# Feed-forward values and the residual stream turned by VectorE in 32x32 blocks instead of by TensorE

## The chip, the cores and the metric

The kernel runs on one core of one Trainium2 chip. The metric is the device time of one execution in microseconds (us). Engines are named as the profile names them: PE is TensorE (PEld its weight loads), DVE is VectorE, ACT is ScalarE, POOL is GpSimd, SP is the engine that issues most DMAs.

## What is computed

An encoder trunk of two layers on 256 tokens of 2048 channels, all in float32. The attention, state-space and pooling parts stand before the output projection and are not touched by the change:

```python
def hybrid_layer(x, norm1_w, w_in, ..., norm2_w, w_gate, w_up, w_down):
    h = rms_norm(x, norm1_w)
    proj = jnp.matmul(h, w_in).astype(jnp.float32)
    ...
    mix = jnp.concatenate([att, ssd, pool], axis=-1).astype(x.dtype)
    x = x + jnp.matmul(mix, w_out)
    h = rms_norm(x, norm2_w)
    ff = jax.nn.silu(jnp.matmul(h, w_gate)) * jnp.matmul(h, w_up)
    return x + jnp.matmul(ff, w_down)
```

After both layers one more RMSNorm gives the output. The feed-forward width is 5632, eleven pieces of 512.

## The kernel before

**Units and halves.** All weights are cut on the host into units of 128 x 2048 numbers (1 MB), in the order in which they are used. `load(i)` brings unit i from memory into one of 3 `raw` buffers. `prep(h)` (line 135) makes half h of a unit, 128x1024, ready: ACT rounds it to the matmul's format (`whi`, L148), DVE computes what the rounding left (`wlo`, L149). Each product is then three matmuls: rounded by rounded (L321), rounded by rest (L322), rest by rounded (L324). So a unit is two halves, and each half is 12 matmuls of 512 columns. `whi` and `wlo` have 5 buffers each: the buffer that half h gives back when its last matmul is through is filled with half h+5, which PE wants four halves later.

**Order of the work.** It is written out by hand. In step i the program issues, engine by engine: the two `prep` of halves 2i+3 and 2i+4, then `evac(i-1)`, which takes the results of the unit before out of PSUM, then unit i's matmuls. Small jobs are put at a place inside a later step with `at(step, fn, pos=k)`; where such a job has PE work, it is slipped in between the matmuls (`side_slot`). Every engine runs its instructions in the order in which they were issued.

**Token units.** Units of kind `out`, `gate`, `up` and `down` go through `mm_token`: the tokens are the stationary operand (two chunks c of 128 tokens), the weights move, and four units (three in the last part of the feed-forward, `PARTS = (4, 4, 3)`) make one result of 256 tokens x 512 channels, with tokens on the partitions. The next matmul needs channels on the partitions, so the result has to be turned:

- after each `up` unit of a group, `ff_up` (L750) multiplies gate and up to `fv`, and `ff_trans` turns it: 8 PE transposes (L759) against an identity into PSUM banks, then ACT (L764) and DVE (L765) split it into rounded part and rest, `ffp`, the operand of `down`. This is done 11 times a layer;
- after each `out` group, and after each `down` group of the last part in layer 0, `residual` (L204) adds the result to `xs`, and `xtrans_feat` turns it in the same way (L218), with the split in `xpair` (L197 on ACT, L198 on DVE) into `xp`, the operand of the next projections. This is done 4 times for each of three residual sums.

The first two `out` groups are held open: three of their four units run first, then the last unit of group 0 and the last unit of group 1 follow each other directly.

Of the kernel before, what the change touches and what calls it, by code (L numbers as in the profile page):

```python
# [15 lines left out]
F32 = mybir.dt.float32  # L19
F32R = mybir.dt.float32r  # L20
AF = mybir.ActivationFunctionType
# [26 lines left out]
def trunk(ctx, tc, xT, xin, wall, par, fin, dsk, plw, cst, dtab, rcnt, out):  # L48
# [22 lines left out]

    def t3(name, dt=F32):
        return ep.tile([128, 3, T], dt, tag="e", name=name)

    def bank(name):
        return auxp.tile([128, 512], F32, tag="aux", name=name)
# [114 lines left out]
    def xpair(k, l, off, v=None):  # L191
# [6 lines left out]
        DVE.scalar_tensor_tensor(t[:, T:], v, w, t[:, :T].bitcast(F32), op0=ALU.mult, op1=ALU.subtract)  # L198
        st["xp"][k] = t

    def residual(n, accs):
        for c in range(2):
            x = xs[c][:, n * 512:n * 512 + 512]
            DVE.tensor_tensor(x, x, accs[c], op=ALU.add)  # L204
# [5 lines left out]
            q = t2("sq")  # L210
            ACT.activation(q, xs[c][:, n * 512:n * 512 + 512], AF.Square, accum_out=st["ssq"][:, c * 4 + n:c * 4 + n + 1])

    def xtrans_feat(n, l, off, half):
        p = bank("xf")
        for b in range(2):
            f = (4 * n + 2 * half + b) * 128
            for c in range(2):
                PE.transpose(p[:, b * T + c * 128:b * T + c * 128 + 128], xs[c][:, f:f + 128], ident)  # L218
                yield
        for b in range(2):  # L220
            xpair(4 * n + 2 * half + b, l, off, p[:, b * T:b * T + T])

    def rstd_cols():
        r = sm.tile([128, T + 4], F32, name="rbc", bufs=1)
# [519 lines left out]
            del st["plw"], st["rc"]  # L744

    def ff_up(f, accs):
        st["fv"] = []
        for c in range(2):
            v = t2("fv")
            DVE.scalar_tensor_tensor(v, accs[c], st["r"][:, T + c:T + c + 1], st["sg"][c], op0=ALU.mult, op1=ALU.mult)  # L750
            st["fv"].append(v)
        del st["sg"]

    def ff_trans(f, half, fv):
        p = bank("ft")
        for b in range(2):
            o = (2 * half + b) * 128
            for c in range(2):
                PE.transpose(p[:, b * T + c * 128:b * T + c * 128 + 128], fv[c][:, o:o + 128], ident)  # L759
                yield  # L760
        for b in range(2):
            t = t2("ffp", F32R)
            v = p[:, b * T:b * T + T]
            ACT.copy(t[:, :T], v)  # L764
            DVE.tensor_tensor(t[:, T:], v, t[:, :T].bitcast(F32), op=ALU.subtract)  # L765
            st["ff", 4 * f + 2 * half + b] = t

    def fin_load():
        st["fw"] = [t2("fw") for _ in range(4)]
# [27 lines left out]
    def evac(i, acc):  # L797
        u = units[i]
        kind, l, j = u["kind"], u["l"], u["j"]
        if kind == "dt":  # L800
            dt_evac(l, acc)
            at(i + 2, dt_exp, l, pos="b")
            at(i + 3, dt_ln, pos="b")
            at(i + 4, dt_fin, pos="a")
            at(i + 5, dt_cols)
            at(i + 7, cumsums)
            st["mix"] = [None] * 16
        elif kind == "xbc":
            conv(l, j, acc)
            at(i + 2, conv_tap0, l, j, pos="c")  # L810
            at(i + 3, conv_taps, l, j, pos="a")
            at(i + 4, conv_silu, l, j, pos="b")
            if j < 8:
                at(i + 5, xtrans, j)
            elif j == 11:
                at(i + 5, cb, 0)
                at(i + 6, cb, 1)
            if j == HEADS_AT:
                b = i + 2
                for h in range(16):  # L820
                    at(b + h - (0 if h == 0 else 1), row_load, h, pos="a")
                    at(b + h + 1, decay, h, pos="a")
                    at(b + h + 1, decay_exp, h, pos="b")
                    at(b + h + 2, gmat, h, pos="b")
                    at(b + h + 3, ymm, h)
                b += 1
                for g in range(2):
                    at(b + 8 * g + 10, gate_skip, l, g, pos="a")
                    at(b + 8 * g + 11, gate_mul, g, pos="c")
                    at(b + 8 * g + 12, gate_norm, g, pos="b")  # L830
                    at(b + 8 * g + 13, gate2, l, g, 0)
                    at(b + 8 * g + 14, gate2, l, g, 1)
        elif kind == "z":
            if j == 3:
                st["ssd"] = {}
            if j % 4 == 3:
                if i == 3:
                    at(i + 2, z_evac, 0, acc, pos="c")
                else:
                    z_evac(j // 4, acc)  # L840
        elif kind == "v":
            if j % 4 == 3:
                v_evac(j // 4, acc)
        elif kind == "qk":
            pair, m = divmod(j, 6)
            qk_evac(pair, m, acc)
            if m == 5:
                b = i + 3 if pair == 0 else i + 2
                for c in range(2):
                    at(b + c, att_a, pair, c, pos=13)  # L850
                    at(b + c + 1, att_n, pair, c, pos="a")
                    for sl in range(2):
                        at(b + c + 1, att_b, pair, sl, c, pos=5)
                    at(b + c + 2, att_c, pair, c, pos=2)
        elif kind == "u":
            if j == 3:
                pass
            pool_evac(j, acc)
            at(i + 2, pool_mm, l, j, pos=11)
        elif kind == "out":  # L860
            residual(j, acc)
            squares(j)
            at(i + 2, xtrans_feat, j, l, P_N2, 0, pos=2)
            at(i + 2, xtrans_feat, j, l, P_N2, 1, pos=10)
            if j == 3:
                at(i + 3, rstd_cols, pos="b")
        elif kind == "gate":
            st["sg"] = []
            for c in range(2):
                s = t2("sg")  # L870
                ACT.activation(s, acc[c], AF.Silu, scale=st["r"][:, T + c:T + c + 1])
                st["sg"].append(s)
        elif kind == "up":
            ff_up(j, acc)
            fv = st.pop("fv")
            at(i + 2, ff_trans, j, 0, fv, pos=2)
            at(i + 2, ff_trans, j, 1, fv, pos=10)
        elif kind == "down":
            residual(j, acc)
            if u["part"] == len(PARTS) - 1:  # L880
                squares(j)
                if l + 1 < L:
                    at(i + 2, xtrans_feat, j, l + 1, P_N1, 0, pos=2)
                    at(i + 2, xtrans_feat, j, l + 1, P_N1, 1, pos=10)
                    if j == 3:
                        at(i + 3, rstd_cols, pos="b")
                        at(i + 4, rstd_rows, pos=2)
                        at(i + 5, rstd_parity, pos=2)
                else:
                    if j == 0:  # L890
                        ACT.activation(warm, epst, AF.Sqrt)
                        fin_load()
                    if j < 3:
                        fin_weight(j)
            if j == 3:
                for f in range(4 * u["f0"], 4 * (u["f0"] + u["nq"])):
                    del st["ff", f]
# [73 lines left out]
    return c, d.astype(np.float32), rc  # L971


def _feature(w):
    k, n = w.shape[0] // 128, w.shape[1] // 128
    return w.reshape(k, 128, n, 128).transpose(2, 1, 0, 3).reshape(n, 128, k * 128)
# [7 lines left out]
def _pack(inp):  # L984
    out = []
    put = lambda a: out.append(np.ascontiguousarray(a).reshape(-1))
    for l in range(L):
        w = inp["w_in"][l]
        q, k, v, z, xbc, dt, u = np.split(w, np.cumsum([ATT, ATT, ATT, INNER, 1536, 32])[:6], axis=1)
        put(_token(z))  # L990
        dtp = np.zeros((D, 128), np.float32)
        dtp[:, :32] = dt
        put(_feature(dtp))
        put(_feature(xbc)[list(CONV_ORDER)])
        put(_token(v))
        qf, kf = _feature(q), _feature(k)
        for p in range(4):
            put(qf[[p, 4 + p, 8 + p]])
            put(kf[[p, 4 + p, 8 + p]])
        put(_feature(u)[::-1])  # L1000
        rows = [None] * KT
        for n in range(8):
            rows[n] = 4 + n
        for n in range(4):
            rows[MIX_ATT[n]] = n
            rows[MIX_POOL[n]] = 12 + n
        o = _token(inp["w_out"][l].reshape(KT, 128, D)[rows].reshape(D, D))
        for n in range(HELD):
            put(o[n][:3])
        for n in range(HELD):  # L1010
            put(o[n][3])
        put(o[HELD:])
        g, up = _token(inp["w_gate"][l]), _token(inp["w_up"][l])
        gu = np.stack([g, up], axis=1)
        f0 = 0
        for n in PARTS:
            put(gu[f0:f0 + n])
            put(_token(inp["w_down"][l][f0 * 512:(f0 + n) * 512]))
            f0 += n
    return np.concatenate(out)  # L1020

# [36 lines left out]
```

## Time and profile before

| what | value |
|---|---|
| time, median of 3 runs | 2465.73 us (2465.63 to 2467.09) |
| the profiled execution's own time | 2464.96 us |
| its span in the trace | 2463.2 us |
| TensorE clock granted, mean | 0.998 |
| PE busy | 2440.2 us, 99% |
| DVE busy | 1427.1 us, 58% |
| ACT busy | 1186.4 us, 48% |
| memory read | 454.43 MB, 185 GB/s over the span |

A row of a group of instructions gives line, engine, operation, what is written and what is read, shapes and count; after the first bar the summed busy time in us and the mean of one in ns; after the second bar the idle time of the engine just before them in us, and what ended it. A row of a timeline gives start in us, length in us, engine, line, operation and count; in brackets the idle time before it and what ended it. A line number is that of the kernel before; the changed kernel's lines are some 4 higher at the top and 27 higher further down.

### The profile page before, as it was taken

To read this page: it belongs to the slowest core of one execution; us is meant where nothing else is said; L and a number is where in the kernel's file an instruction comes from. 1 tells how busy PE (TensorE), PEld (TensorE's weight loads), DVE (VectorE), ACT (ScalarE), POOL (GpSimd) and SP (SyncE) were. 2 spreads that over 40 slices of the span, in tenths; PEclk is the share of its full clock that TensorE was granted. 3 is DMA by queue.
4 is the path that set the end of the run, shared out by engine and by line. 5 is a ranking of instruction groups with operands and counts; after the bars stand their busy time and mean duration, and the time that the engine had idled before them with its cause. 6 is when DMAs were issued, how large, how long until landed. Compare 5 with 4: busy or idle time off the path is not lost.

```text
span 2463.2 us, 30214 instructions
## 1 busy us (share of the span) xinstructions
PE 2440.2 (99%) x11954; PEld 2029.4 (82%) x11954; DVE 1427.1 (58%) x1791; ACT 1186.4 (48%) x1610; POOL 238.1 (10%) x329
## 2 busy tenths in 40 slices
PE   8999999999999999999999999999999999999997
PEld 7888888888888888888888888888888888888886
DVE  6787765555454555545558787655545545454454
ACT  6576554544444444344555755445544444444443
POOL 2175002000000000000001830020000000000001
PEclk9999999999999999999999999999999999999999
DMA  7565544455555555555454654445555555555553
GB/s 271 200 220 171 175 153 155 172 204 188 188 188 196 193 185 194 189 188 190 173 201 157 225 180 155 165 160 188 187 190 188 188 193 187 194 193 191 188 200 125
DMA packets 67103, 458.57 MB, mean 186 GB/s; under 512 B 7776, under 2 KB 7920, under 8 KB 13328
## 3 DMA queue, kind: packets, MB, share of 16 engines
q1 hardware_dynamic: 63360, 445.27, 50.6%
q0 software_dynamic: 3456, 11.09, 1.6%
q8 instruction: 94, 1.54, 0.3%
q14 instruction: 49, 0.40, 0.0%
q10 hardware_dynamic: 144, 0.26, 0.0%
HBM read 454.43 MB, written 2.16 MB: 185 GB/s over the span
## 4 chain that ended last, share of the span: by engine, by line
PE 98%; DVE 1%; ACT 0%; issue 0%; DMA 0%; POOL 0%; SPq 0%; DVEq 0%; ACTq 0%; POOLq 0%
PE acc L321 25%; PE acc L324 25%; PE acc L322 25%; PE acc L286 11%; PE acc L288 6%; PE ft L759 1%; PE acc L291 1%; PE sc L649 1%; PE op L688 1%; PE pt L673 1%; PE y L569 0%; PE y L567 0%; PE xf L218 0%; DMA raw<-wall 0%; DVE s L656 0%
## 5 line engine op out<-in xcount | busy, mean ns | idle before, releaser
L149 DVE TENSOR_TENSOR wlo<-raw,whi 128x1024 fp32r<-128x1024 f32 (+1 forms) x839 | 1028.0, 1234 | 846.9 <-ACT whi L148 845.7
L148 ACT CAST whi<-raw 128x1024 fp32r<-128x1024 f32 (+1 forms) x839 | 873.5, 1049 | 976.9 <-PE acc L324 832.9
L321 PE MATMUL acc<-whi,xp 128*128 128x512 f32 x1728 | 685.8, 397 | 8.4 <-ACT whi L148 8.4
L324 PE MATMUL acc<-whi,xp 128*128 128x512 f32 x1728 | 685.5, 397 | 0.0
L322 PE MATMUL acc<-wlo,xp 128*128 128x512 f32 x1728 | 674.8, 391 | 0.0
L286 PE MATMUL acc<-xp,whi 128*128 128x512 f32 x1230 | 458.3, 409 | 0.0
L321 PEld LDWEIGHTS acc<-whi,xp 128*128 128x128 f32 x1728 | 326.0, 189 | 77.5 <-ACT whi L148 8.4
L324 PEld LDWEIGHTS acc<-whi,xp 128*128 128x128 f32 x1728 | 326.0, 189 | 70.9
L322 PEld LDWEIGHTS acc<-wlo,xp 128*128 128x128 f32 x1728 | 326.2, 189 | 63.6 <-DVE wlo L149 0.4
L288 PE MATMUL acc<-xp,wlo 128*128 128x256 f32 x1312 | 367.2, 290 | 0.0
L324 PE MATMUL acc<-whi,ffp 128*128 128x512 f32 x704 | 277.3, 394 | 0.0
L321 PE MATMUL acc<-whi,ffp 128*128 128x512 f32 x704 | 277.3, 394 | 0.0
L322 PE MATMUL acc<-wlo,ffp 128*128 128x512 f32 x704 | 274.1, 389 | 0.0
L286 PEld LDWEIGHTS acc<-xp,whi 128*128 128x128 f32 x1230 | 231.3, 188 | 50.4 <-issue 3.2
L288 PEld LDWEIGHTS acc<-xp,wlo 128*128 128x128 f32 x1312 | 248.2, 189 | 14.5 <-issue 0.8
L324 PEld LDWEIGHTS acc<-whi,ffp 128*128 128x128 f32 x704 | 132.2, 188 | 29.5
L321 PEld LDWEIGHTS acc<-whi,ffp 128*128 128x128 f32 x704 | 132.2, 188 | 28.6
L322 PEld LDWEIGHTS acc<-wlo,ffp 128*128 128x128 f32 x704 | 132.3, 188 | 26.2
L451 POOL TENSOR_TENSOR pad<-cd,rbc 128x256 f32<-128x256 f32 x24 | 18.7, 781 | 1019.8 <-DVE cd L274 1019.8
L324 PE MATMUL acc<-whi,mix 128*128 128x512 f32 x256 | 102.7, 401 | 0.0
L321 PE MATMUL acc<-whi,mix 128*128 128x512 f32 x256 | 102.1, 399 | 0.0
L322 PE MATMUL acc<-wlo,mix 128*128 128x512 f32 x256 | 99.8, 390 | 0.0
(183 smaller groups left out, 1584.1 us busy)
## 6 DMA issues: line engine op xcount, KB each, us to landing
raw<-wall SPq DMA_DIRECT2D x417, 1024.0 KB, 4.8
rowb<-rowd POOLq DMA_DIRECT2D x32, 256.0 KB, 3.7
xt<-xT SPq DMA_DIRECT2D x8, 256.0 KB, 7.7
xs<-xin SPq DMA_DIRECT2D x2, 1024.0 KB, 7.9
out<-xs SPq DMA_DIRECT2D x5, 256.0 KB, 3.4
raw<-wall SPq DMA_DIRECT2D x4, 256.0 KB, 5.9
rc<-rcnt POOLq DMA_DIRECT2D x4, 256.0 KB, 5.8
fw<-fin POOLq DMA_DIRECT2D x4, 256.0 KB, 3.6
```

The lines of the kernel that those rows point to most:

```text
L148: ACT.copy(hi[:, c:e], r)
L149: DVE.tensor_tensor(lo[:, c:e], r, hi[:, c:e].bitcast(F32), op=ALU.subtract)
L286: PE.matmul(acc, lhsT=hi, rhs=rhs, start=first, stop=False)
L288: PE.matmul(acc[:, T:], lhsT=lo, rhs=rhs[:, :T], start=False, stop=False)
L291: PE.matmul(acc, lhsT=hi, rhs=rhs, start=False, stop=True)
L321: PE.matmul(a, lhsT=xh, rhs=hi[:, s], start=first, stop=False)
L322: PE.matmul(a, lhsT=xh, rhs=lo[:, s], start=False, stop=False)
L324: PE.matmul(a, lhsT=xl, rhs=hi[:, s], start=False, stop=last)
L649: PE.matmul(p[sl][:, o:o + n], lhsT=q[a, m, c::2], rhs=k[a, m] if m == 0 else k[a, m, c::2], start=True, stop=True)
L673: PE.transpose(p[:, b * 128:b * 128 + 128], s[:, b * 128:b * 128 + 128], ident)
L688: PE.matmul(p[64 * sl:64 * sl + 64, c * 128:c * 128 + 128], lhsT=vs[b][:, h:h + 64], rhs=pt[sl][:, b * 128:b * 128 + 128], start=(b == 0), ...
L759: PE.transpose(p[:, b * T + c * 128:b * T + c * 128 + 128], fv[c][:, o:o + 128], ident)
```

## The change

The 32x32 block transpose of DVE takes the place of the PE transposes for `fv` and `xs`. `move` copies a 128x512 tile by 16 instructions: number (a, b) reads partitions 32a to 32a+31, columns 128b to 128b+127, turns its four 32x32 blocks, and writes partitions 32b to 32b+31, columns 128a to 128a+127. That leaves the channels of each group of 512 in another order on the partitions, and the rows of `w_in`, `w_gate`, `w_up` and `w_down`, the two norm weights and the first input `xT` are put into the same order on the host (`_order`). The transposed tile lies in SBUF, in a buffer of the pool `ep`, and the split into rounded part and rest reads it there, in pieces of 128x128 (four runs of 32 columns) instead of 128x256 from PSUM.

```diff
+    def t3f(name):
+        return t3(name).rearrange("p a b -> p (a b)")[:, :512]
...
+    def move(v, d):
+        for a in range(4):
+            for b in range(4):
+                DVE.transpose(d[32 * b:32 * b + 32, 128 * a:128 * a + 128],
+                              v[32 * a:32 * a + 32, 128 * b:128 * b + 128])
+
+    def turned(d, m):
+        return d.rearrange("p (a m j) -> p m a j", a=4, m=4)[:, m]
+
+    def cols(t):
+        return t.rearrange("p (a j) -> p a j", a=4)
...
-    def xtrans_feat(n, l, off, half):
-        p = bank("xf")
-        for b in range(2):
-            f = (4 * n + 2 * half + b) * 128
-            for c in range(2):
-                PE.transpose(p[:, b * T + c * 128:b * T + c * 128 + 128], xs[c][:, f:f + 128], ident)
-                yield
-        for b in range(2):
-            xpair(4 * n + 2 * half + b, l, off, p[:, b * T:b * T + T])
+    def x_turn(n):
+        st["xd", n] = [t3f("xd") for _ in range(2)]
+        for c in range(2):
+            move(xs[c][:, n * 512:n * 512 + 512], st["xd", n][c])
+
+    def x_split(n, l, off, half):
+        if n == 0 and half == 0:
+            st["xp"] = [None] * KT
+        for m in (2 * half, 2 * half + 1):
+            k = 4 * n + m
+            t = t2("xp", F32R)
+            w = pr[:, l, off + k:off + k + 1]
+            for c in range(2):
+                v = turned(st["xd", n][c], m)
+                hi, lo = (cols(t[:, o + c * 128:o + c * 128 + 128]) for o in (0, T))
+                ACT.activation(hi, v, AF.Copy, scale=w)
+                DVE.scalar_tensor_tensor(lo, v, w, hi.bitcast(F32), op0=ALU.mult, op1=ALU.subtract)
+            st["xp"][k] = t
+        if half:
+            del st["xd", n]
...
     def ff_up(f, accs):
-        st["fv"] = []
+        st["fd"] = []
         for c in range(2):
             v = t2("fv")
             DVE.scalar_tensor_tensor(v, accs[c], st["r"][:, T + c:T + c + 1], st["sg"][c], op0=ALU.mult, op1=ALU.mult)
-            st["fv"].append(v)
+            d = t3f("fd")
+            move(v, d)
+            st["fd"].append(d)
         del st["sg"]
 
-    def ff_trans(f, half, fv):
-        p = bank("ft")
...
+    def ff_split(f, half):
+        for m in (2 * half, 2 * half + 1):
+            t = t2("ffp", F32R)
+            for c in range(2):
+                v = turned(st["fd"][c], m)
+                hi, lo = (cols(t[:, o + c * 128:o + c * 128 + 128]) for o in (0, T))
+                ACT.copy(hi, v)
+                DVE.tensor_tensor(lo, v, hi.bitcast(F32), op=ALU.subtract)
+            st["ff", 4 * f + m] = t
+        if half:
+            del st["fd"]
...
         elif kind == "out":
             residual(j, acc)
             squares(j)
-            at(i + 2, xtrans_feat, j, l, P_N2, 0, pos=2)
-            at(i + 2, xtrans_feat, j, l, P_N2, 1, pos=10)
+            x_turn(j)
+            at(i + 2, x_split, j, l, P_N2, 0, pos=2)
+            at(i + 2, x_split, j, l, P_N2, 1, pos=8)
...
+def _order(n):
+    f = np.arange(n).reshape(n // 512, 4, 4, 32)
+    return f.transpose(0, 2, 1, 3).reshape(n)
```

`down` of the last part in layer 0 is changed as `out` is. Where DVE's order moves is shown at two places. First, DVE around one `up` result in the steady part of the feed-forward (`wlo` is the rest of a weight half, `fv` the product of gate and up, `fd` the turned tile, `ffp` its rest). Before:

```order
L149 TENSOR_TENSOR wlo<-raw,whi 128x1024 x12
L750 SCALAR_TENSOR_TENSOR fv<-acc,rbc,sg 128x512 x2
L149 TENSOR_TENSOR wlo<-raw,whi 128x1024 x2
L765 TENSOR_TENSOR ffp<-ft,ffp 128x256 x4
L149 TENSOR_TENSOR wlo<-raw,whi 128x1024 x14
```

With the change:

```order
L153 TENSOR_TENSOR wlo<-raw,whi 128x1024 x12
L777 SCALAR_TENSOR_TENSOR fv<-acc,rbc,sg 128x512
L208 STREAM_TRANSPOSE fd<-fv 32x128 x16
L777 SCALAR_TENSOR_TENSOR fv<-acc,rbc,sg 128x512
L208 STREAM_TRANSPOSE fd<-fv 32x128 x16
L153 TENSOR_TENSOR wlo<-raw,whi 128x1024 x2
L790 TENSOR_TENSOR ffp<-fd,ffp 128x128 x8
L153 TENSOR_TENSOR wlo<-raw,whi 128x1024 x14
```

The 32 block transposes stand ahead of the next `wlo`, in one run that only the second `fv` parts.

Second, DVE where the first two `out` groups end one unit apart (`xs` is the residual sum, `xd` the turned tile, `xp` its rest). Before:

```order
L204 TENSOR_TENSOR xs<-xs,acc 128x512 x2
L149 TENSOR_TENSOR wlo<-raw,whi 128x1024 x2
L204 TENSOR_TENSOR xs<-xs,acc 128x512 x2
L198 SCALAR_TENSOR_TENSOR xp<-xf,pr,xp 128x256 x4
L149 TENSOR_TENSOR wlo<-raw,whi 128x1024 x2
L198 SCALAR_TENSOR_TENSOR xp<-xf,pr,xp 128x256 x4
L149 TENSOR_TENSOR wlo<-raw,whi 128x1024 x6
```

With the change:

```order
L220 TENSOR_TENSOR xs<-xs,acc 128x512 x2
L208 STREAM_TRANSPOSE xd<-xs 32x128 x32
L153 TENSOR_TENSOR wlo<-raw,whi 128x1024 x2
L220 TENSOR_TENSOR xs<-xs,acc 128x512 x2
L208 STREAM_TRANSPOSE xd<-xs 32x128 x32
L245 SCALAR_TENSOR_TENSOR xp<-xd,pr,xp 128x128 x8
L153 TENSOR_TENSOR wlo<-raw,whi 128x1024 x2
L245 SCALAR_TENSOR_TENSOR xp<-xd,pr,xp 128x128 x8
L153 TENSOR_TENSOR wlo<-raw,whi 128x1024 x6
```

Two runs of 32 block transposes now have only two `wlo` between them. On PE the 176 transposes of L759 and the 96 of L218 are gone; nothing else is.

## Rows read from the trace of the kernel before

**Rows 1.** The page's busy times: engine, busy us, share of the span, instructions.
```profile
PE 2440.2 (99%) x11954; PEld 2029.4 (82%) x11954; DVE 1427.1 (58%) x1791; ACT 1186.4 (48%) x1610; POOL 238.1 (10%) x329
```
**Rows 2.** The page's chain that ended last, by engine.
```profile
PE 98%; DVE 1%; ACT 0%; issue 0%; DMA 0%; POOL 0%; SPq 0%; DVEq 0%; ACTq 0%; POOLq 0%
```
**Rows 3.** All waits of PE: engine, line, what for, total us, times, longest us.
```profile
PE acc L321 <- ACT whi L148: 8.4, 1, 8.4
PE pt L673 <- DVE s L666: 1.8, 4, 0.8
```
**Rows 4.** Timeline of PE around the first transposes of a feed-forward tile.
```profile
548.85 0.39 PE L322 MATMUL acc<-wlo,xp 128*128 128x512 f32 x1
...
549.53 0.40 PE L322 MATMUL acc<-wlo,xp 128*128 128x512 f32 x1
549.77 0.27 PE L759 MATMUL ft<-cs,fv 128*128 128x128 f32 x1
...
550.11 0.27 PE L759 MATMUL ft<-cs,fv 128*128 128x128 f32 x1
...
550.45 0.39 PE L322 MATMUL acc<-wlo,xp 128*128 128x512 f32 x1
```
**Rows 5.** The groups of PE, those that the change takes away.
```profile
L759 PE MATMUL ft<-cs,fv 128*128 128x128 f32 x176 | 47.7, 271 | 0.0
...
L218 PE MATMUL xf<-cs,xs 128*128 128x128 f32 x96 | 26.0, 271 | 0.0
```
**Rows 6.** The groups of DVE by shape, those that price the added and moved work.
```profile
L149 DVE TENSOR_TENSOR wlo<-raw,whi 128x1024 fp32r<-128x1024 f32 x835 | 1025.2, 1236 | 844.7 <-ACT whi L148 843.6
...
L750 DVE SCALAR_TENSOR_TENSOR fv<-acc,rbc,sg 128x512 f32<-128x512 f32 x44 | 30.9, 743 | 0.0
...
L548 DVE SCALAR_TENSOR_TENSOR e<-e,dcol,cbm 128x128 f32<-128x128 f32 x64 | 21.7, 378 | 0.0
...
L641 DVE TENSOR_TENSOR qk<-cd,rbc 128x256 f32<-128x256 f32 x24 | 10.2, 425 | 0.8
...
L508 DVE COPY xs<-xt 128x128 f32<-128x128 f32 x16 | 4.6, 287 | 7.5 <-ACT xs L507 7.3
...
L490 DVE TENSOR_TENSOR cbm<-cb,cs 128x128 f32<-128x128 f32 x4 | 1.1, 281 | 0.0
...
L384 DVE TENSOR_SCALAR dta<-dta 32x256 f32<-32x256 f32 x2 | 0.5, 274 | 0.0
```
**Rows 7.** Timeline of DVE from the end of an up result on.
```profile
545.15 1.23 DVE L149 TENSOR_TENSOR wlo<-raw,whi 128x1024 fp32r<-128x1024 f32 x1 [1.50 <-ACT whi L148]
546.29 1.40 DVE L750 SCALAR_TENSOR_TENSOR fv<-acc,rbc,sg 128x512 f32<-128x512 f32 x2
547.88 1.23 DVE L149 TENSOR_TENSOR wlo<-raw,whi 128x1024 fp32r<-128x1024 f32 x1 [0.18 <-ACT whi L148]
```
**Rows 8.** Timeline of ACT in the same stretch.
```profile
544.07 1.05 ACT L148 CAST whi<-raw 128x1024 fp32r<-128x1024 f32 x1 [1.67 <-PE acc L324]
546.78 1.06 ACT L148 CAST whi<-raw 128x1024 fp32r<-128x1024 f32 x1 [1.67 <-PE acc L324]
```
**Rows 9.** Timeline of ACT at the end of the first out group.
```profile
447.60 1.05 ACT L148 CAST whi<-raw 128x1024 fp32r<-128x1024 f32 x1 [1.67 <-PE acc L324]
```
**Rows 10.** Timeline of DVE at the end of the first out groups.
```profile
449.83 1.28 DVE L204 TENSOR_TENSOR xs<-xs,acc 128x512 f32<-128x512 f32 x2
...
461.13 2.36 DVE L149 TENSOR_TENSOR wlo<-raw,whi 128x1024 fp32r<-128x1024 f32 x2 [0.45 <-ACT whi L148]
```
**Rows 11.** Timeline of DVE in the last down of layer 0: two residual sums.
```profile
1182.88 1.28 DVE L204 TENSOR_TENSOR xs<-xs,acc 128x512 f32<-128x512 f32 x2
...
1200.22 1.28 DVE L204 TENSOR_TENSOR xs<-xs,acc 128x512 f32<-128x512 f32 x2
```
**Rows 12.** The groups of ACT: a cast of a weight half, and a 128x128 piece.
```profile
L148 ACT CAST whi<-raw 128x1024 fp32r<-128x1024 f32 x835 | 871.0, 1051 | 974.7 <-PE acc L324 832.9 <-PE acc L291 79.2 <-PE acc L286 41.9
...
L533 ACT ACTIVATE e<-rowb,nbias 128x128 f32<-128x128 f32 x32 | 12.7, 398 | 0.1
```
**Rows 13.** The page's DMA issues: the weights, KB each, median us from issue to landing.
```profile
raw<-wall SPq DMA_DIRECT2D x417, 1024.0 KB, 4.8
```

More of the change, by code (lines that the diff above doesn't have):

```diff
@@ L750, in ff_up @@
             DVE.scalar_tensor_tensor(v, accs[c], st["r"][:, T + c:T + c + 1], st["sg"][c], op0=ALU.mult, op1=ALU.mult)
-            st["fv"].append(v)
+            d = t3f("fd")
+            move(v, d)
+            st["fd"].append(d)
         del st["sg"]
-    def ff_trans(f, half, fv):
-        p = bank("ft")
-        for b in range(2):
-            o = (2 * half + b) * 128
+    def ff_split(f, half):
+        for m in (2 * half, 2 * half + 1):
+            t = t2("ffp", F32R)
             for c in range(2):
[L759 to L766, printed above, removed]
+                v = turned(st["fd"][c], m)
[5 more added lines that the diff above has]
+            del st["fd"]
     def fin_load():
@@ L874, in evac @@
             ff_up(j, acc)
-            fv = st.pop("fv")
-            at(i + 2, ff_trans, j, 0, fv, pos=2)
-            at(i + 2, ff_trans, j, 1, fv, pos=10)
+            at(i + 2, ff_split, j, 0, pos=2)
+            at(i + 2, ff_split, j, 1, pos=8)
         elif kind == "down":
@@ L882, in evac @@
                 if l + 1 < L:
-                    at(i + 2, xtrans_feat, j, l + 1, P_N1, 0, pos=2)
-                    at(i + 2, xtrans_feat, j, l + 1, P_N1, 1, pos=10)
+                    x_turn(j)
+                    at(i + 2, x_split, j, l + 1, P_N1, 0, pos=2)
+                    at(i + 2, x_split, j, l + 1, P_N1, 1, pos=8)
                     if j == 3:
@@ L987, in _pack @@
     for l in range(L):
-        w = inp["w_in"][l]
+        w = inp["w_in"][l][_order(D)]
         q, k, v, z, xbc, dt, u = np.split(w, np.cumsum([ATT, ATT, ATT, INNER, 1536, 32])[:6], axis=1)
@@ L1012, in _pack @@
         put(o[HELD:])
-        g, up = _token(inp["w_gate"][l]), _token(inp["w_up"][l])
+        g, up = _token(inp["w_gate"][l][_order(D)]), _token(inp["w_up"][l][_order(D)])
         gu = np.stack([g, up], axis=1)
@@ L1017, in _pack @@
             put(gu[f0:f0 + n])
-            put(_token(inp["w_down"][l][f0 * 512:(f0 + n) * 512]))
+            put(_token(inp["w_down"][l][f0 * 512:(f0 + n) * 512][_order(n * 512)]))
             f0 += n
@@ L1032, in cols @@
             return a.reshape(-1, 128).T
-        par[:, l, P_N1:P_N1 + 16] = cols(inp["norm1_w"][l])
-        par[:, l, P_N2:P_N2 + 16] = cols(inp["norm2_w"][l])
+        par[:, l, P_N1:P_N1 + 16] = cols(inp["norm1_w"][l][_order(D)])
+        par[:, l, P_N2:P_N2 + 16] = cols(inp["norm2_w"][l][_order(D)])
         par[:, l, P_CW:P_CW + 60] = inp["conv_w"][l].reshape(5, 12, 128).transpose(2, 1, 0).reshape(128, 60)
@@ L1043 @@
     arrays = dict(
-        xT=np.ascontiguousarray(inp["x"][0].reshape(T, KT, 128).transpose(2, 1, 0)),
+        xT=np.ascontiguousarray(inp["x"][0][:, _order(D)].reshape(T, KT, 128).transpose(2, 1, 0)),
         xin=inp["x"][0].reshape(2, 128, D), wall=wall, par=par,
```

## Prediction

> **What bounds the kernel now.** I read the busy times first: PE is busy for 99% of the span, DVE for 58%, ACT for 48% [rows 1]. A busy share alone says little, so the chain that ended last comes next: 98% of it is PE [rows 2]. Third, the waits of PE: one of 8.4 us at the start and four of 1.8 us together [rows 3]. In 2463 us PE never waits for a `wlo` of DVE. So PE's stream of matmuls is the time, and whatever leaves it comes off, as long as DVE keeps delivering `wlo`. DVE's own order therefore has to be read at the places where the change puts work into it.
>
> **What leaves PE.** Three matmuls without a transpose take 549.53 - 548.85 = 0.68 us; the next three, with two transposes among them, 550.45 - 549.53 = 0.92 us [rows 4]. So a transpose costs PE 0.12 us, not the 271 ns of its row, which overlap its neighbours. 176 + 96 = 272 go [rows 5]: 272 x 0.119 = 32.4 us. ACT no longer waits for PE before a split; it was not on the chain.
>
> **What DVE gets.** 22 `fv` tiles and 12 residual sums, each 32 instructions of 32x128: 1088 block transposes. No row shows one. Call p the time from one start to the next.
> - Duration: the nearest rows are one-source instructions that pass 128 elements, the copy of 128x128 at 287 ns, and the one on 32 partitions, 32x256, at 274 ns [rows 6]. I take 287.
> - Overlap: two independent `fv` of 743 ns take 1.40 us together [rows 7], so 0.086 us overlap. A multiply that needs its predecessor's result starts 0.8 / 24 = 0.033 us after its end (L641) [rows 6]. Each block transpose writes other partitions than the one before, by the code; all DVE work of before starts at partition 0, so every overlap that the trace shows is within one place.
>
> The ends are p = 0.274 - 0.086 = 0.19 and 0.287 + 0.035 = 0.322. I take no overlap, since only instructions at one place are seen to overlap, and the middle of 0.287 and 0.322: **p = 0.305 us**, 9.76 us for 32. The Trainium skill, VectorE: DVE Perf Modes, section Two Vector instructions with no wait between them, says that an instruction whose output starts in another group of 32 partitions than the last output starts only when everything before it has finished. No run here shows it yet. By that rule p is a whole duration; without it p falls to the overlap's price and the sum to that of the first rival. The same page, section The three transpose paths, gives 311 ns for a 128x128 transpose in bf16 on VectorE; with it as p the sum below would be 43 us, an estimate.
>
> **How late DVE may be.** A half lasts 546.78 - 544.07 = 2.71 us, say 2.72 [rows 8]. Its buffer is refilled when it is through, PE wants it four halves later, and `wlo` one matmul after `whi`: 10.88 + 0.23 = 11.1 us for a cast of 1.05 and a subtraction of 1.23. Times below are from T, the end of the result's last unit, in the schedule without stalls.
>
> 1. *An `up` result, 20 times.* DVE starts `fv` at 546.29 - 544.07 = T+2.22 [rows 7, 8]. Two `fv`, each now followed by transposes that wait for it: 2 x 0.78 = 1.56. Then 32p = 9.76, to T+13.54. The next `wlo`, at 547.88 before, ends at T+14.8; its half came free at T+2.72, so it is due at T+13.83. PE stalls 0.98 us; 20 x 0.98 = 19.6. Afterwards DVE, which idles 1.5 us in every half, catches up within the eight units.
> 2. *The last `up` of a part of three, twice.* `down` wants this tile in its third unit, T+10.88, and the rest 0.45 later: T+11.33. DVE has it at 13.54 + two `wlo` 2.4 + the first piece 0.28 (as L490) [rows 6] = T+16.2. Stall 4.9; 9.8 together.
> 3. *The first two `out`, twice.* T is 447.60, the residual starts at T+2.23 and takes 1.28 [rows 9, 10]. In order: 1.32 + 32p, two `wlo` 2.4 (2.36 for two [rows 10]), 1.32 + 32p, eight pieces of `xp` at 0.378 - 0.08 = 0.30 [rows 6], 2.4, and a `wlo`, 1.23: T + 10.9 + 64p = T+30.4. That `wlo` came free at T+8.16 and is due at T+19.27. Stall 11.1; 22.3 together.
> 4. *The other two `out`, four times.* DVE has 8 `wlo` at 1.18, 1.28, 9.76 and 2.4 = 22.9 in 8 halves of 2.72 = 21.8: 1.1 each, 4.4.
> 5. *The last `down` of layer 0.* Residuals are 1200.22 - 1182.88 = 17.3 us apart [rows 11], 16.3 without the 8 transposes. DVE's work for each: 6 x 1.18 + 1.28 + 9.76 + 2.4 = 20.5. DVE is the bound: 3 x 4.2, and 0.7 for the first, 13.3.
>
> Stalls: 19.6 + 9.8 + 22.3 + 4.4 + 13.3 = 69.4 us. **Sum: 69.4 - 32.4 = +37 us.** The profiled execution took 2464.96 us, so 2502; the median of the runs shown is 0.8 us higher, which changes nothing. Above p = 0.274 every site is exposed, and 1 ns on p is 1.09 us.
>
> **What is costed at nothing.** ACT: eight pieces of at most 398 ns in place of four [rows 12], 3.2 us an `up`. They wait for the transposes, and the next casts queue behind them on ACT: last piece at about T+16.4, cast to T+17.5, its `wlo` at T+18.8, due T+19.27. ACT's 975 us of waiting for PE [rows 12] cover it; without that cover it is up to 3 us a tile. DVE's pieces (8 x 0.2 for 4 x 0.42) change little. SP: a `raw` buffer comes back when DVE's second `wlo` of its unit is done, at T+14.8 here; 4.8 us of landing [rows 13] make T+19.6, and that half's cast is wanted at T+24.9, so 5 us cover it. POOL gets nothing. PSUM: the second accumulator is read 5 us later, and its buffer is wanted at T+21.7. Reordered weight rows are the same bytes in the same loads.
>
> **The rivals.** *Transposes overlap* (faster). DVE would start one while the last drains, and p is 0.19 to 0.205. Then site 1 is covered, and at 0.205 the others give 2 x 1.7 + 2 x 4.7 + 3 x 1.0 = 15.8: 2449, at 0.19 2444; with nothing exposed 2433, the floor. For it: independent DVE instructions do overlap [rows 7]. Against it: none of them changes partitions. 22%.
>
> *In between*: p from 0.205 to 0.287, by a shorter duration or half an overlap. At 0.274 the stalls are 1 (site 1) + 8 + 18 + 0.4 + 10 = 37: +5. The sign turns at about p = 0.27. 2449 to 2482; 10%.
>
> *Longer transposes*: a block can be written only once it is read, and if the four blocks do not follow each other without a gap, p can reach two copies' worth, 0.57, and 2502 + 1.09 x 265 = 2791; at 0.42 it is 2627. Nothing in the trace excludes it; the price per element of every one-source row speaks against. 13%.
>
> *The change does not do what it says*: PE loses its 272 instructions but no time, if they lay in the shadow of weight loads. Then 2502 + 32 = 2534. Rows 4 speak against it, 0.92 against 0.68; I give it no chance of its own.
>
> **How the numbers follow.** No overlap with p from 0.287 to 0.322: 2482 to 2521, 55%; its middle is the forecast, 2502. Range: from 2440, which takes in most of the overlap case, to 2535 (p = 0.335), which takes in the lower end of the long one; some 15% lie outside. A measurement of this kernel tells about 0.2%, 5 us, from no change. Faster: the overlap's 22% and half of the case in between, 27%. Within: 5%. Slower: 68%.
>
> **What would show it.** A row of 1088 block transposes, its mean and its starts: p of 0.287 or more, start to start. PE's waits: `acc` for `wlo`, absent before, some 20 of about 1 us, two clusters of about 11 us, a wait of about 5 us for `ffp` twice, and 3 x 4 us near 1200 us. PE's busy time lower by some 32 us, less what busy counts while stalled. DVE's busy share near 70%. The clock stays at 1.0: the stalls are short. I am wrong if transposes start less than 0.25 us apart, if DVE's lateness is made up before PE needs the half, or if a single block transpose takes over 0.34 us.

## The result, and the profile after

The changed kernel is slower: 2534.8 us median (2534.1 to 2539.0) against 2465.8, a ratio of 1.028 (95% interval 1.0265 to 1.030). The forecast had the sign and the place, but about half of the loss: +37 us, where +69 was measured.

The busy times and the chain, which answer to [rows 1] and [rows 2] (engine, busy us, share, instructions; then shares of the chain):

```profile
PE 2432.5 (96%) x11682; PEld 2017.3 (80%) x11682; DVE 1747.2 (69%) x3015; ACT 1194.8 (47%) x1746; POOL 239.6 (9%) x329
...
PE 76%; DVE 20%; ACT 2%; issue 2%; DMA 1%; POOL 0%; SPq 0%; ACTq 0%; DVEq 0%; POOLq 0%
```

DVE is busy for 320 us more and has 20% of the chain that ended last, where it had 1%. PE is busy for only 8 us less, though it has 272 instructions less. All waits of PE, which answer to [rows 3] (what for, total us, times, longest us):

```profile
PE acc L349 <- DVE wlo L153: 64.7, 33, 8.9
PE acc L351 <- DVE ffp L790: 10.6, 2, 5.3
PE acc L348 <- ACT whi L152: 9.7, 3, 7.9
PE pt L700 <- DVE s L693: 1.8, 4, 0.8
PE rr L262 <- DVE rbc L255: 1.3, 1, 1.3
```

PE never waited for `wlo` before; now it does 33 times. The timeline of DVE around one `up` result shows why; it answers to [rows 7]:

```profile
558.10 1.22 DVE L153 TENSOR_TENSOR wlo<-raw,whi 128x1024 fp32r<-128x1024 f32 x1 [1.49 <-ACT whi L152]
559.25 0.74 DVE L777 SCALAR_TENSOR_TENSOR fv<-acc,rbc,sg 128x512 f32<-128x512 f32 x1
560.02 5.05 DVE L208 STREAM_TRANSPOSE fd<-fv 32x128 f32<-32x128 f32 x16
565.11 0.75 DVE L777 SCALAR_TENSOR_TENSOR fv<-acc,rbc,sg 128x512 f32<-128x512 f32 x1
565.89 5.05 DVE L208 STREAM_TRANSPOSE fd<-fv 32x128 f32<-32x128 f32 x16
570.98 2.36 DVE L153 TENSOR_TENSOR wlo<-raw,whi 128x1024 fp32r<-128x1024 f32 x2
```

The next `wlo` starts 12.9 us after the last one, at 570.98; before, it started 2.7 us after it. 16 block transposes take 5.05 us, so 0.316 us from start to start. The groups give a mean of 303 ns for one, so there is no overlap, and 13 ns lie between the end of one and the start of the next:

```profile
L208 DVE STREAM_TRANSPOSE fd<-fv 32x128 f32<-32x128 f32 x704 | 213.2, 303 | 10.5
L208 DVE STREAM_TRANSPOSE xd<-xs 32x128 f32<-32x128 f32 x384 | 116.2, 303 | 5.3
```

The second loss was not in the forecast. The mean granted clock is 0.988, against 0.998 before. These are the stretches in which TensorE was granted 0.50 of its clock, its lower level of 1.2 GHz, apart from the end of the program (stretch, its length, PE busy and instructions, granted clock, DMA share and rate):

```profile
471.97:482.21 10.24, 4.61 (x11) 0.50 0.30 102
1199.01:1205.84 6.83, 5.46 (x13) 0.50 0.69 236
1243.39:1246.80 3.41, 3.40 (x8) 0.50 0.64 211
1263.87:1267.28 3.41, 3.41 (x9) 0.50 0.73 247
1284.35:1287.76 3.41, 3.41 (x10) 0.50 0.77 281
1731.49:1745.14 13.65, 6.05 (x14) 0.50 0.24 83
1789.52:1792.93 3.41, 3.41 (x9) 0.50 0.74 267
2461.94:2468.77 6.83, 4.48 (x11) 0.50 0.55 176
sum 51.19, PE 34.22; mean PE 4.28
```

The first of them lies around the longest stall. On PE's timeline the matmul at 477.60 ends a wait of 8.86 us; those behind it start 0.43 us apart, and from 482.35 on 0.23 us apart again, as in [rows 4]:

```profile
477.60 0.80 PE L349 MATMUL acc<-wlo,mix 128*128 128x512 f32 x1 [8.86 <-DVE wlo L153]
...
480.33 0.63 PE L349 MATMUL acc<-wlo,mix 128*128 128x512 f32 x1
480.76 0.63 PE L351 MATMUL acc<-whi,mix 128*128 128x512 f32 x1
...
482.35 0.40 PE L348 MATMUL acc<-whi,mix 128*128 128x512 f32 x1
482.59 0.39 PE L349 MATMUL acc<-wlo,mix 128*128 128x512 f32 x1
```

PE worked 34.2 us in these stretches, work that takes 17.1 us at the upper level by the ratio of the clocks (by the distances of the matmuls above, 0.43 and 0.23 us, 18.3, so that some 16 us are lost). The account of the two spans, 2533.4 - 2463.2 = 70.2 us:

| term | us | from |
|---|---|---|
| waits of PE, 88.1 against 10.2 before | +77.9 | the sums of the waits, after and [rows 3] |
| 38 waits more, each 0.16 longer than its row | +6.2 | a wait is counted from the end of the matmul before, 0.39 after its start; undisturbed, the next starts 0.23 after it |
| work at the lower clock level | +17.1 | half of 34.2 |
| 272 PE transposes less | -32.4 | the forecast's term; the sixth experiment gives 34 |
| sum | +68.8 | of 70.2 |

### The profile page after: what moved, and what is told of

The parts are those of the page before. It is cut to its first block, busy times and chain, and to the rows that moved or that the text cites. A ratio compares the mean times of both kernels' runs of the same rounds, so it can differ in the third digit from the quotient of the medians.

```text
span 2533.4 us, 30928 instructions
## 1 busy us (share of the span) xinstructions
PE 2432.5 (96%) x11682; PEld 2017.3 (80%) x11682; DVE 1747.2 (69%) x3015; ACT 1194.8 (47%) x1746; POOL 239.6 (9%) x329
## 4 chain that ended last, share of the span: by engine, by line
PE 76%; DVE 20%; ACT 2%; issue 2%; DMA 1%; POOL 0%; SPq 0%; ACTq 0%; DVEq 0%; POOLq 0%
PE acc L349 18%; PE acc L351 18%; PE acc L348 18%; PE acc L313 11%; DVE fd L208 8%; PE acc L315 6%; DVE xd L208 4%; DVE wlo L153 4%; ACT whi L152 1%; DVE fv L777 1%; DMA raw<-wall 1%; PE acc L318 1%; DVE xp L245 1%; PE sc L676 1%; DVE xs L220 1%
## 5 line engine op out<-in xcount | busy, mean ns | idle before, releaser
L208 DVE STREAM_TRANSPOSE fd<-fv 32x128 f32<-32x128 f32 x704 | 213.2, 303 | 10.5
L351 PEld LDWEIGHTS acc<-whi,ffp 128*128 128x128 f32 x704 | 134.2, 191 | 39.3 <-DVE ffp L790 11.4
L208 DVE STREAM_TRANSPOSE xd<-xs 32x128 f32<-32x128 f32 x384 | 116.2, 303 | 5.3
```

The costliest lines, as they stand in the source:

```text
L208: DVE.transpose(d[32 * b:32 * b + 32, 128 * a:128 * a + 128], v[32 * a:32 * a + 32, 128 * b:128 * b + 128])
L351: PE.matmul(a, lhsT=xl, rhs=hi[:, s], start=False, stop=last)
```

## The experiments

Theory: a block transpose that reads or writes other partitions than the one before it starts only when that one has finished, so 32 of them hold DVE for 10.1 us; the `wlo` behind them is late, PE stalls, and behind its longer idle times TensorE works at the lower level. Rivals: the rate is the instruction's own; the loss comes with DVE's load as such, in proportion to the number of block transposes; the lower clock costs nothing. Each run was compared with runs of the kernel before on the same chip, whose medians are 2465.4 to 2465.8 us. Diffs are excerpts, against the changed kernel; those of the fifth experiment are against the kernel before.

### 1. The feed-forward alone, and the residual sums alone

```diff
 e1_ff_only: as before the change again
-            x_turn(j)
-            at(i + 2, x_split, j, l, P_N2, 0, pos=2)
-            at(i + 2, x_split, j, l, P_N2, 1, pos=8)
+            at(i + 2, xtrans_feat, j, l, P_N2, 0, pos=2)
+            at(i + 2, xtrans_feat, j, l, P_N2, 1, pos=10)
...
 e2_x_only: as before the change again
             ff_up(j, acc)
-            at(i + 2, ff_split, j, 0, pos=2)
-            at(i + 2, ff_split, j, 1, pos=8)
+            fv = st.pop("fv")
+            at(i + 2, ff_trans, j, 0, fv, pos=2)
+            at(i + 2, ff_trans, j, 1, fv, pos=10)
```

> Only the 22 feed-forward tiles go through the block transposes; the residual sums stay on TensorE. Theory (the time is PE stalls behind late wlo, less 0.119 us for each PE transpose, plus work at the lower clock level after stalls): 20 stalls of 1.6 us, 2 of 5.4 us with about 2.5 us each of work at the lower level behind them, less 176 x 0.119 = 20.9: 2466 + 32 + 11 + 5 - 21 = 2493 us. Rival (the loss is in the contention of DVE for the whole run and scales with the number of block transposes, 704 of 1088): 2466 + 0.65 x 69 = 2511 us.

> Only the 12 residual sums go through the block transposes; the feed-forward stays on TensorE. Theory: the stalls of the changed kernel around the out groups and the last down of layer 0, about 40 us, and some 9 us of work at the lower clock level, less 96 x 0.119 = 11.4: 2466 + 40 + 9 - 11 = 2504 us. Rival (in proportion to the number, 384 of 1088): 2466 + 0.35 x 69 = 2490 us.

Measured: 2494.7 us (ratio 1.0118, 1.0103 to 1.0134) and 2509.1 us (1.0176, 1.0161 to 1.0191). So, net of the PE transposes that they replace, the 384 block transposes of the residual sums cost 43.5 us and the 704 of the feed-forward 29 us; a loss in proportion to their number would be the other way round. Where they stand decides. The waits of PE in the first of the two show the forecast's two sites, 20 of 1.45 us and 2 of 5.3 us:

```profile
PE acc L338 <- DVE wlo L153: 29.8, 21, 1.5
PE acc L340 <- DVE ffp L779: 10.6, 2, 5.3
```

The second came 5 us above the expectation: its lower-clock stretches sum to 44 us (55.7 in all, less 11.4 at the end of the program), of which PE worked in about 31, some 16 us lost where 9 were expected. One of them, 3.4 us long, lies 18 us after the start, ahead of all block transposes, so about 14 us belong to the change.

### 2. What keeps one block transpose from overlapping the next

```diff
 e3_read_first
-        for a in range(4):
-            for b in range(4):
+        for b in range(4):
+            for a in range(4):
...
 e4_same_group
-                DVE.transpose(d[32 * b:32 * b + 32, 128 * a:128 * a + 128],
+                DVE.transpose(d[32 * a:32 * a + 32, 128 * b:128 * b + 128],
                               v[32 * a:32 * a + 32, 128 * b:128 * b + 128])
```

> The two loops of move change places: the partitions read now differ from one block transpose to the next, the partitions written only at every fourth. Theory (a change of either keeps the next one from starting early): start to start stays 0.316 us and the time 2535 within 4 us. Rival (only a change of the written partitions does): 12 of 16 start 0.08 to 0.1 us earlier, 0.24 us on average, and the time falls to about 2455 us.

> Every block transpose writes the partitions it reads, and four follow each other on the same partitions; the turned tiles hold other numbers than the product needs. Theory: 12 of 16 overlap with the one before by about 0.08 us, so their distance is 0.22 us and the mean about 0.245 us, below the 0.265 us from which an up result stalls PE; time about 2455 us. Rival (0.316 us is the rate of the instruction itself, whatever it writes): 0.316 us and 2535 us.

Measured: 2535.2 us (1.0286, 1.0269 to 1.0303), as the changed kernel, and 2458.6 us (0.9971, 0.9960 to 0.9983). Sixteen block transposes on DVE's timeline, first with the loops exchanged, then within the same partitions:

```profile
559.63 5.06 DVE L208 STREAM_TRANSPOSE fd<-fv 32x128 f32<-32x128 f32 x16
```

```profile
552.11 3.58 DVE L208 STREAM_TRANSPOSE fd<-fv 32x128 f32<-32x128 f32 x16
```

With the loops exchanged 12 of 16 write the same partitions as the one before and read others; with the change 12 of 16 read the same and write others. The two runs of 16 take 5.06 and 5.05 us, so either change is enough. Where neither changes for 12 of 16, the run takes 3.58 us, and the loss is gone (the blocks stay on the partitions where they were, so only the time of this run is read). This run has the same number of the same instructions as the changed kernel: it is neither their rate nor their number that costs, but that each waits for the one before.

### 3. Both chunks from one place to one place in pairs

```diff
...
+        for n in part:
+            a, b = divmod(n, 4)
+            for c in range(2):
+                DVE.transpose(d[c][32 * b:32 * b + 32, 128 * a:128 * a + 128],
+                              v[c][32 * a:32 * a + 32, 128 * b:128 * b + 128])
...
```

> The block transposes of both token chunks from one place to one place follow each other, so every second one reads and writes the partitions of the one before. Theory: those start after about 0.22 us, the others after 0.316, so 32 take 8.6 us instead of 10.1. Stalls fall by 1.5 us for each tile: about 0.1 at 20 up results, 3.9 at the two last ones, some 8 at each pair of out groups, 33 us in all, and the clock drops after fewer of them: 2466 + 33 - 32 + 10 = 2477 us. Rival (only the number of instructions counts): 2535 us.

Measured: 2467.0 us (1.0008, 0.9999 to 1.0018): no difference from the kernel before, and 10 us better than expected. All 32 now take 8.14 us, where 8.6 were expected:

```profile
552.08 8.14 DVE L209 STREAM_TRANSPOSE fd<-fv 32x128 f32<-32x128 f32 x32
```

The first four of them, one row each:

```profile
552.08 0.29 DVE L209 STREAM_TRANSPOSE fd<-fv 32x128 f32<-32x128 f32 x1
552.30 0.26 DVE L209 STREAM_TRANSPOSE fd<-fv 32x128 f32<-32x128 f32 x1
552.57 0.30 DVE L209 STREAM_TRANSPOSE fd<-fv 32x128 f32<-32x128 f32 x1
552.81 0.26 DVE L209 STREAM_TRANSPOSE fd<-fv 32x128 f32<-32x128 f32 x1
```

The second of a pair starts about 0.24 us after the first, 0.06 us before its end, and its own row is shorter, 0.26 us; so the next pair, which waits for that end, starts 0.27 us later and not 0.316. Most of these block transposes write other partitions than they read, as in the changed kernel, and every second one still overlaps, so it is the change from one instruction to the next that counts.

PE waits for `wlo` 6 times, the longest 6.9 us after the first two `out` groups. The 20 waits after `up` results are gone, since 8.14 us keep the next `wlo` just within its time. So 2 us less in a run of 10 give back 68 us, the work at the lower clock among them. The 10 us against the expectation divide about evenly. All waits of PE sum to 36.7 us, 26.5 more than before, or 28.6 with 0.16 for each of 13 waits more, where 33 were expected. PE works 10.5 us at the lower level, 5.2 us lost, where 10 were expected.

### 4. Does the idle time of PE lower the clock, and does that cost anything

```diff
+    def fill(n):
+        p = bank("fill")
+        for _ in range(n):
+            PE.matmul(p, lhsT=ident, rhs=cs[:, :512], start=True, stop=True)
...
+            if j == 1:
+                at(i + 2, fill, 20, pos=8)
...
+            if j == 10:
+                at(i + 3, fill, 12, pos=0)
```

> Matmuls on constants that nobody reads are put on TensorE where it stands idle longest: 20 of 0.43 us each in the 8.9 us stall after the first two out groups, 12 in the 5.3 us stall after the last up of a part of three, in both layers. The output is unchanged. Theory (idle time is what lowers the clock, and work behind the stall at the lower level costs some 17 us in all, 10 of it behind these four): the clock stays up there and the time falls by 6 to 10 us, to 2525 to 2529. Rival (the lower level costs nothing, or does not hang on the idle time): 2535 or a few us more.

Measured: 2548.7 us (1.0339, 1.0321 to 1.0356), 14 us more than the changed kernel. The expectation was wrong because of the price of the filling: one such matmul takes two entries of 0.43 us in the trace, so 20 and 12 of them filled 17.4 and 10.4 us, 27 us more in the two layers than stood idle. The trace of this run still tells theory and rival apart. It has 128 entries of filling 0.43 us apart, 54.9 us; the waits of PE fall from 88.1 to 57.7 us, and there are 7 fewer, 0.16 us each, so without any effect of the clock the span would grow by 23.4 us. PE's work at the lower level falls from 34.2 to 13.1 us, worth 10.5, which leaves 12.9; the spans differ by 12.9 (2546.3 and 2533.4). The run was repeated with 10 and 6:

> As the run before it with matmuls on constants, but half as many: 10 and 6, since each of those took 0.87 us and the run filled 17.4 and 10.4 us where 8.9 and 5.3 us stood idle. Now 8.7 and 5.2 us are filled. Theory (idle time lowers the clock): the stalls stay as long as in the changed kernel, no lower level behind these four, 10 to 13 us less: 2522 to 2525 us. Rival (the lower level costs nothing, or does not hang on the idle time): 2535 us.

Measured: 2528.6 us (1.0256, 1.0241 to 1.0272), 6 us less than the changed kernel, although PE has 64 more entries of work that nobody needs. The lower-clock stretches, in the view used above:

```profile
504.43:507.84 3.41, 3.41 (x10) 0.50 0.65 271
1241.71:1245.12 3.41, 3.41 (x9) 0.50 0.73 250
1262.19:1265.60 3.41, 3.41 (x10) 0.50 0.80 274
1282.67:1286.08 3.41, 3.41 (x10) 0.50 0.87 308
1736.64:1740.05 3.41, 2.85 (x7) 0.50 0.50 154
sum 17.05, PE 16.49; mean PE 3.30
```

PE's work at the lower level falls from 34.2 to 16.5 us, worth 8.9 us. The filling (64 entries 0.43 us apart, 27.5 us) and the idle time left (61.4 us) sum to 0.8 us more than the idle time of the changed kernel, and five waits fewer, 0.16 us each, take that back; so 8.9 us should be gone, and the spans differ by 7.2 (2533.4 and 2526.2). It fell short of the 10 to 13 us expected because two lower stretches stood where none was expected. The filling began one half before the longest stall, and 2.7 us of idle time were left behind it; in the second layer, at 1737 us, the clock fell after them, in the first, at 479 us, it did not. The stretch at 504 us lies behind a stall of 2.1 us after the third `out` group, where the changed kernel has one of 1.1 us. So idle time of PE lowers the clock, and the work behind it pays.

### 5. A version that spreads the block transposes

Only feed-forward tiles, in pairs, half of the 32 one step later, except at the last `up` of a part of four, where all 32 stay together; the last `up` of the part of three and all residual sums stay on PE:

```diff
...
+            if j == 10:
+                at(i + 2, ff_trans, j, 0, fv, pos=2)
+                at(i + 2, ff_trans, j, 1, fv, pos=10)
+            else:
+                ff_move(0, fv)
+                late = j not in (3, 7)
+                if late:
+                    at(i + 2, ff_move, 1, fv, pos="b")
+                else:
+                    ff_move(1, fv)
+                at(i + 2 + late, ff_split, j, 0, pos=2)
+                at(i + 2 + late, ff_split, j, 1, pos=8)
...
```

> Only feed-forward tiles, without the last one of a part of three, in pairs as in the run before, and half of the 32 one step later, so that one wlo is never behind more than 16 of them (the last tile of a part of four keeps all 32 together, since it is wanted earlier); residual sums and the two last tiles stay on TensorE. Theory: no wlo is late, and 160 PE transposes less are 160 x 0.119 = 19 us: 2446.6 us. Rival (DVE's load itself slows the matmuls, through the memory that both read): less than half of it, above 2456 us.

Measured: 2445.2 us (0.9918, 0.9904 to 0.9933), 20.5 us faster than the kernel before. All waits of PE:

```profile
PE acc L338 <- ACT whi L152: 7.8, 1, 7.8
PE pt L690 <- DVE s L683: 1.9, 4, 0.8
PE acc L339 <- DVE wlo L153: 0.5, 1, 0.5
```

The waits are those of [rows 3] again, with one of 0.5 us for `wlo` more, and the clock is 0.998. DVE is busy for 1577 us, 150 more than before, and PE does not lose by it. The third and fourth `out` sum can go the same way:

```diff
...
+            if j >= 2:
+                x_turn(j)
+                at(i + 2, x_split, j, l, P_N2, 0, pos=2)
+                at(i + 2, x_split, j, l, P_N2, 1, pos=8)
...
```

> The version with spread feed-forward tiles, and the residual sums of the third and fourth out group through the block transposes as well, in pairs. Theory: DVE has about 21.0 us of work there in 21.8, so no stall, and 32 PE transposes less: 2445.2 - 3.8 = 2441 us. Rival (DVE is full there, and a late wlo or a late weight load takes the gain): 2445 us or more.

Measured: 2441.0 us (0.9900, 0.9884 to 0.9917), as expected, and the fastest version here that computes the whole: 24 us faster than before, 94 us faster than the change.

### 6. What the PE transposes cost by themselves

```diff
-        for a in range(4):
-            for b in range(4):
-                DVE.transpose(d[32 * b:32 * b + 32, 128 * a:128 * a + 128],
-                              v[32 * a:32 * a + 32, 128 * b:128 * b + 128])
+        DVE.tensor_copy(d, v)
```

> Each run of 16 block transposes is replaced by one copy of the 128x512 tile on DVE, so the products get numbers that were not turned; everything else is as in the changed kernel. Theory: no stall is left and the 272 PE transposes are gone, 272 x 0.119 = 32.4 us: 2433 us. Rival (the transposes lay in the shadow of weight loads or the smaller split pieces cost PE time): 2450 us or more.

Measured: 2431.3 us (0.9863, 0.9848 to 0.9877), 34 us less than before; the tiles are copied and not turned, so again only the time is read. The term of 32.4 us holds, and neither the smaller split pieces nor their strided reading cost PE anything.

## Why the prediction was right in its kind and wrong in its size

- **The gain on PE** (272 x 0.119 = 32.4 us, from the distance of matmuls in [rows 4]) was right: 34 us by the sixth experiment.
- **No overlap between block transposes** was right, and for the reason given: experiments 2 and 3 show it. The price is 0.316 us where each one changes partitions, against 3.58 / 16 = 0.22 us on average where three of four have the partitions of the one before. The rule that the prediction names from the Trainium skill (VectorE: DVE Perf Modes, section Two Vector instructions with no wait between them) agrees with the traces: one that changes partitions starts 13 ns after the end of the one before, one that does not starts about 0.06 us before that end. The Trainium skill's figure for a 128x128 transpose in bf16 (VectorE: DVE Perf Modes, section The three transpose paths) is 311 ns; the 32x128 one in f32 takes 303 ns here.
- **The price p** was 0.305 us, chosen as the middle of 0.287 and 0.322. Measured: 0.316, by 303 ns and 13 ns of distance. At 1.09 us for each ns that is 12 us of the 32 missed, and the forecast's own sum with it would be +49.
- **The stalls, site by site**, were right within 6 us each. With p = 0.316 the sum gives 69.4 + 12.0 = 81.4 us; measured are 77.9 + 6.2 = 84.1. After an `up` result 1.45 + 0.16 us, where the sum gives 1.33; at the last tile 5.3, where it gives 5.2. By site, with 0.16 us for each wait: 32.2 us after the `up` results, where the sum with p = 0.316 gives 26.6; 10.9 at the last `up` of a part of three (10.5); 22.5 at the first two `out` (23.7); 6.9 at the other two (5.8); 10.9 at the last `down` of layer 0 (14.7). So the sums agree better than the sites, because two of them miss in opposite directions.
- **The step that failed is the sentence "The clock stays at 1.0: the stalls are short."** It priced the time behind a stall at nothing. Eight stretches at the lower level cost 16 to 17 us, and experiment 4 shows that they hang on the idle time: where it is filled, they go, and the work behind it takes less time. With p and this term the forecast would have been +66, of 69 measured. The measured time is also the upper edge of the range, 2535 us, but that edge stands for p = 0.335, which did not come true.
- **Costed at nothing** held for POOL, PSUM and the reordered rows. For SP it held only in part: in the changed kernel ACT waits 87 us in all for weights (`raw`) whose buffer DVE gave back late, though PE waits only 1.3 us more for `whi` than before.
- **The rivals**: overlap needs equal partitions, which the change never has; a block transpose of two copies' length is excluded by 303 ns; that the PE transposes lie in the shadow of weight loads is excluded by experiment 6, so its 2534 us meet the measured time by chance.

## What to carry to other kernels

An engine with 42% of idle time can still be too slow: what counts is the longest run of work that is put ahead of something the bounding engine waits for, against the lead that the buffers give. The same operation, ordered in pairs, split over two steps and left out where the lead is short, turned a loss of 69 us into a gain of 24. A stall of TensorE of some us should be priced with the work behind it at the lower clock, 3.4 to 6 us of it behind a stall of 2 to 9 us in this trace, which costs half of that.

## What the runs showed that was not expected

In the changed kernel a lower-clock stretch came behind idle times of 2.0 to 8.9 us, but not behind all of the short ones: of the 2.0 us waits near 527 and 1789 us only the second had one, and none of the 20 waits of 1.45 us, which are 45 us or more apart, did. What decides between two equal waits these runs do not show. Filling idle time with matmuls that nobody reads made the kernel 6 us faster, though in a kernel without the stalls there is nothing to fill.
